# Weight ring below the phase buffers, chained first loads, gate by groups, score matrices inside the mixers, a last tile in halves and a retuned ordering model, on eight Trainium2 cores

## The chip, the cores and the metric

The kernel runs on all 8 cores of one Trainium2 chip (trn2), which lie on two dies (cores 0 to 3 and 4 to 7). Each core computes its own share of the tokens, and no core waits for another. The metric is device microseconds (us) of the slowest core. An execution can fall into a slow state, in which the cores of a die show a lower granted clock (0.83 to 0.98 in the slow runs here, where the others show 0.98 to 0.99). Such runs are named as slow here and are left out of every comparison.

## The reference, cut to what matters

```python
D_MODEL = 1024; SEQ = 8192; BATCH = 2; N_MEM = 256; D_FF = 2816
h = x
for i in range(2):
    n = rms_norm(h, g_mix[i])
    if i == 0:      # A: GLU -> conv over 31 positions -> LayerNorm -> silu; B: gated conv over 3
        h = h + conv_pair_mixer(n, ev_w_in, ..., ev_w_out)
    else:           # u, v = split(gelu(n @ w_in)); y = u * (w_s . layer_norm(v) + b_s); y @ w_out
        h = h + chunked_sgu_mixer(n, od_w_in, ..., od_w_out)
    mem_n = rms_norm(mem, g_mem[i])
    h = h + memory_cross_attention(rms_norm(h, g_xattn[i]), mem_n, w_q, w_k, w_v, w_o)
    h = h + swiglu(rms_norm(h, g_ffn[i]), w_gate, w_up, w_down)
return rms_norm(h, g_final)
```

The attention works on 256 memory tokens, so the kernel folds the query weights into the keys: G = w_q times K, its "score matrix", is built once for each layer, and each token tile multiplies by G.

## The kernel before

Each core holds 2048 tokens in four tiles of 512 (`hT_63` to `hT_66` in the trace; their normalized copies are `nT_67` to `nT_70`). The program is recorded as a list of operations for five engines. A small ordering model then simulates the list and fixes the order on each engine. At run time each engine works strictly in that order.

```python
class Prog:
    AHEAD = {"pe": 6, "act": 32, "dve": 32, "pool": 1, "sp": 1}   # how far an engine may look ahead
    DMA_RATE = 190e3                       # assumed transfer rate, bytes per us
...
            o = min((o for o in go if o.ready <= t + self.SLIP), key=lambda o: (o.due, o.n))
...
            if o.dma is None:
                free[e] = t + o.cost
            else:
                link = max(link, t + 0.8) + o.cost / self.DMA_RATE
                o.done = link + 1.2
```

Weights come as slabs of 512 KB or 1 MB into a ring of memory that lies above the buffers of the running phase. When it is full, it starts again at the phase's border. Slabs are issued from the software queue (POOL), x and small pieces from a hardware queue (SP).

```python
    def ld(self, name, layer, c0):
        ...
        if self.r_ptr + n > SB_LIMIT:
            self.r_ptr = self.r_lo          # border of this phase
...
    def run(...):
        self.load_x(0, "a")                 # all of x at once, halo after tile 0
        for tt in range(1, NT):
            self.load_x(tt, "a")
        self.first_norms()
...
        # conv mixer: LayerNorm and silu write yst; small transfers regroup it as yA
        self.want(("ln", 0))
        self.load_x(1, "b")                 # residual of the later tiles, fetched again
        self.load_x(2, "b")
        self.vproj(0)
...
        # gate of layer 1: tile by tile
        for tt in range(NT):
            for g in range(8):
                ...                         # 4 small matmuls with w_sT, 8 with od_in, gelu, product
        self.kproj(1)
        self.vproj(1)
```

The softmax here doesn't subtract the row's maximum and nothing guards it: scores larger than these inputs give would overflow.

## Time and profile before

| | before |
|---|---|
| time, median of fast runs | 1710.79 us (1709.89 to 1714.03, 4 runs) |
| slowest core of the profiled run | core 4, 1710.6 us |
| TensorE busy | 1592.4 us, 93% |
| table loads on ScalarE | 46, 59.0 us |
| clock granted to the eight cores | 0.981 to 0.985 |

The page's first part gives busy time for each engine. The slices show where TensorE is not full, the windows put numbers on such a stretch, and the list of waits names the tile that TensorE stood still for and what delivered it. In that list, "ACT sqp" and "DVE sqp" are squares from ScalarE and VectorE, which TensorE sums for a norm, and "DMA" is a transfer. The prediction shows these lines.

### The profile page before, as it was taken

The page shows a single profiled execution, that of the slowest core. Times are in us where ns is not written, and L with a number is a line of the kernel's source. Part 1 is how long each engine was busy: PE and PEld are TensorE (multiplying, and loading weights), DVE is VectorE, ACT ScalarE, POOL GpSimd, SP SyncE. Part 2 cuts the span into 40 slices and gives each one's busy share as a digit, 9 for nine tenths or more (in the row PEclk, how much of TensorE's full clock was granted, in tenths as well). Part 3 has the DMA queues.
Part 4 walks back from the last instruction along what each step waited for, and adds up shares of the span by engine and source line. Part 5 has one row for each costly group of instructions (what it writes and reads, how often), then busy time and mean ns, then how long its engine had stood idle before and what let it go on. Part 6 is the DMA issues. An engine that isn't in the chain of part 4 may idle for free.

```text
span 1710.6 us, 23810 instructions; the slowest of 8 cores (1693.8 to 1710.6 us)
## 1 busy us (share of the span) xinstructions
PE 1592.4 (93%) x7799; PEld 752.4 (44%) x7826; DVE 1013.7 (59%) x1636; ACT 708.2 (41%) x1176; POOL 70.1 (4%) x147
## 2 busy tenths in 40 slices
PE   3899895999999999999999897999999999999995
PEld 1444482444444444444444344454444444444442
DVE  1528853665788357673656762474589447683555
ACT  3723364355555043550535422345545134461342
POOL 1000000000000000000000001000000000000000
PEclk9999897999999999999999899999999999999998
DMA  9252248260034355443441208152024436465432
GB/s 202 86 103 38 38 68 192 62 108 4 1 73 82 68 90 96 74 82 66 90 90 25 50 1 133 28 87 50 1 38 80 80 65 121 74 153 118 74 63 99
DMA packets 32376, 130.64 MB, mean 76 GB/s; under 512 B 3584, under 2 KB 10112, under 8 KB 25472
## 3 DMA queue, kind: packets, MB, share of 16 engines
q0 software_dynamic: 18432, 100.03, 33.1%
q1 hardware_dynamic: 13824, 29.08, 5.7%
q8 instruction: 66, 1.08, 0.3%
q14 instruction: 54, 0.44, 0.1%
HBM read 216.51 MB, written 8.39 MB: 131 GB/s over the span
## 4 chain that ended last, share of the span: by engine, by line
PE 84%; DMA 6%; DVE 3%; ACT 3%; issue 2%; SPq 1%; DVEq 0%; ACTq 0%; POOLq 0%
PE ps L595 60%; PE ps L593 21%; DMA hT_65<-x_in 2%; PE ps L107 2%; DMA wbuf_186<-w_od_out 1%; DMA yA_75<-yst 1%; ACT L107 1%; PE ps L1043 1%; DMA wbuf_134<-w_xo 1%; DVE wd L107 1%; DMA wbuf_176<-w_od_in 1%; PE ps L740 1%; DMA wbuf_181<-w_xk 1%; DMA wbuf_175<-w_od_in 1%; SPq L110 0%
## 5 line engine op out<-in xcount | busy, mean ns | idle before, releaser
L107 ACT ACTIVATE ps<-ps 128x512 f32<-128x512 f32 x88 | 50.6, 580 | 216.2 <-PE ps L595 216.1
L595 PE MATMUL ps<-pT,VW 128*128 128x512 f16 x512 | 118.7, 379 | 2.6 <-DVE pT L107 2.6
L107 DVE TENSOR_TENSOR hT_63<-hT_63,ps 128x512 f32<-128x512 f32 x64 | 44.0, 687 | 113.5 <-PE ps L595 111.8
L593 PE MATMUL ps<-tw,sw 128*128 128x512 f16 x352 | 83.5, 379 | 0.8 <-ACT ps L107 0.8
L595 PE MATMUL ps<-tw,sw 128*128 128x512 f16 x352 | 83.5, 379 | 0.6 <-DVE w_0_95 L107 0.6
L107 DVE TENSOR_TENSOR hT_65<-hT_65,ps 128x512 f32<-128x512 f32 x64 | 43.9, 686 | 61.2 <-PE ps L595 61.2
L595 PEld LDWEIGHTS ps<-pT,VW 128*128 128x128 f16 x512 | 50.0, 98 | 63.5 <-issue 3.9
L107 ACT ACT_TABLE_LOAD x46 | 59.0, 1283 | 35.1 <-DVE small L107 10.7
L107 DVE TENSOR_TENSOR hT_64<-hT_64,ps 128x512 f32<-128x512 f32 x64 | 43.9, 685 | 45.9 <-PE ps L595 45.4
L107 DVE TENSOR_TENSOR hT_66<-hT_66,ps 128x512 f32<-128x512 f32 x64 | 43.9, 686 | 45.6 <-PE ps L595 43.5
L107 ACT ACTIVATE pT<-ps,epsc 128x512 f16<-128x512 f32 x64 | 43.7, 683 | 33.1 <-PE ps L595 32.7
L593 PEld LDWEIGHTS ps<-tw,sw 128*128 128x128 f16 x352 | 34.3, 98 | 42.7 <-issue 1.7
L595 PEld LDWEIGHTS ps<-tw,sw 128*128 128x128 f16 x352 | 34.3, 98 | 42.5 <-issue 1.5
L107 ACT ACTIVATE t_2_61<-ps 128x512 f32<-128x512 f32 (+1 forms) x57 | 33.1, 582 | 46.4 <-PE ps L595 41.9
L107 DVE SCALAR_TENSOR_TENSOR nT_67<-hT_63,vec,rs_57 128x512 f16<-128x512 f32 x48 | 34.1, 747 | 28.2 <-ACT sqp_51 L107 26.9
L107 ACT ACTIVATE t_0_59<-ps 128x512 f32<-128x512 f32 (+1 forms) x54 | 31.4, 581 | 40.4 <-PE ps L595 33.2
L595 PE MATMUL ps<-X,wd 128*128 128x256 f16 x288 | 39.3, 285 | 3.6 <-DVE b_ph L107 2.4
L107 DVE TENSOR_TENSOR w_2_97<-ps,w_2_97 128x512 f32<-128x512 f32 x29 | 20.0, 690 | 37.9 <-ACT w_2_97 L107 25.9
L593 PE MATMUL ps<-nT_68,sw 128*128 128x512 f16 x176 | 41.9, 379 | 0.0
L593 PE MATMUL ps<-nT_70,sw 128*128 128x512 f16 x176 | 41.6, 379 | 0.0
L107 DVE TENSOR_TENSOR w_0_95<-ps,w_0_95 128x512 f32<-128x512 f32 x30 | 20.7, 689 | 35.1 <-ACT w_0_95 L107 19.7
L107 DVE TENSOR_TENSOR w_4_99<-ps,w_4_99 128x512 f32<-128x512 f32 x29 | 20.0, 690 | 31.7 <-PE ps L593 16.8
(1249 smaller groups left out, 3371.1 us busy)
## 6 DMA issues: line engine op xcount, KB each, us to landing
hT_64<-x_in SPq DMA_DIRECT2D x8, 512.0 KB, 22.4
hT_65<-x_in SPq DMA_DIRECT2D x8, 512.0 KB, 29.0
hT_66<-x_in SPq DMA_DIRECT2D x8, 512.0 KB, 16.3
X<-a_ph SPq DMA_DIRECT2D x16, 130.0 KB, 6.5
hT_63<-x_in SPq DMA_DIRECT2D x4, 512.0 KB, 10.1
out<-hT_63 SPq DMA_DIRECT2D x4, 512.0 KB, 3.0
out<-hT_64 SPq DMA_DIRECT2D x4, 512.0 KB, 9.9
out<-hT_65 SPq DMA_DIRECT2D x4, 512.0 KB, 3.3
```

Of the source, the lines that this page charges most:

```text
L107: return self.add(eng, lambda e: getattr(e, meth)(**kw), reads, writes, cost=_op_cost(eng, kw))
L593: ins = e.matmul(out, lhsT=l, rhs=r, start=False, stop=(i == np_ - 1), skip_group_check=True)
L595: ins = e.matmul(out, lhsT=l, rhs=r, start=(i == 0), stop=(i == np_ - 1))
L740: ins = e.matmul(self.ps[b][:, i * NMEM:(i + 1) * NMEM], lhsT=ws[i][0](k), rhs=mn[:, k, :], start=(k == 0), stop=(k == KC - 1))
L1043: ins = e.matmul(self.ps[b][:, i * NMEM:(i + 1) * NMEM], lhsT=w(c), rhs=self.kT[:, c, :], start=(hc == 0), stop=(hc == 1))
```

## The change

It is meant to bring data earlier, and to leave TensorE with other work where they are late. It has these parts:

- **Ring:** phase buffers are packed at the top of memory and the ring lies below them from one fixed start. `od_in` is split into `od_v` and `od_u`, and two `od_u` slabs go where K and V of layer 0 were.
- **Start:** the first loads are chained (tile 0, then slabs, then tiles 1, 2, 3). The first four column blocks run chunk by chunk, and VectorE squares every second chunk.
- **yA:** the second fetch of x waits until yA has landed.
- **Gate:** group by group over all tiles, with the K projection in the middle.
- **Scores:** G is built inside the mixers' output projections.
- **Tail:** the last down projection goes tile by tile, the last tile in two halves.
- **Ordering model:** another assumed rate, table loads counted, and table switches put off.

Smaller edits go with these: the norm of the last tile in both mixers is queued after 5 blocks instead of 16, and the attention's products of V and w_o start one step later.

The core of the diff, cut:

```diff
-    DMA_RATE = 190e3
+    TABLES = {AF.Exp: "exp", AF.Ln: "exp", AF.Sigmoid: "sigmoid", AF.Silu: "silu", AF.Gelu_apprx_tanh: "gelu"}
+    TABLE_LOAD = 1.3
+    SWITCH = 4.0
+    DMA_RATE = 320e3
...
-                o = min((o for o in go if o.ready <= t + self.SLIP), key=lambda o: (o.due, o.n))
+                o = min((o for o in go if o.ready <= t + self.SLIP),
+                        key=lambda o: (o.due + (self.SWITCH if o.table not in (None, table) else 0.0), o.n))
...
+                if o.table not in (None, table):
+                    table = o.table
+                    free[e] += self.TABLE_LOAD
...
-        if self.r_ptr + n > SB_LIMIT:
-            self.r_ptr = self.r_lo
+            if self.r_ptr + n > self.r_hi:
+                self.r_ptr = self.r_lo
...
-        for tt in range(1, NT):
-            self.load_x(tt, "a")
+        sl = [self.slab("ev_in", 0, c, None, [self.hT_s[0][2]] if c == 0 else ())[1] for c in (0, 4, 2, 6)]
+        self.load_x(1, "a", [sl[2]])
+        self.load_x(2, "a", [self.hT_s[1][4]])
+        self.load_x(3, "a", [self.hT_s[2][4]])
...
+                if i == 3:
+                    self.load_x(1 + nh, "b", [self.yA_s[nh]])
...
-        self.load_x(1, "b")
-        self.load_x(2, "b")
...
+        for q in range(2):
+            self.slab("od_u", 0, 2 * q, self.kv_lo + q * KC * NMEM * 2)
...
-        for tt in range(NT):
-            for g in range(8):
+        for g in range(4):
+            gate_u(g)
         self.kproj(1)
+        for g in range(4, 8):
+            gate_u(g)
...
+                self.g_step(1, tt, m)      # quarter of G after (1,7), (2,3), (2,7), (3,3)
...
+            if final and h == 1 and part == 1:
+                self.last_down(l, tts, nf) # tile 2 whole, tile 3 in two halves of 256
```

## The prediction

> **What bounds the kernel now.** I read part 1 of the profile page, then the slices, then a table of windows cut at the stage borders, then the list of waits on TensorE and, for the two ends, the timeline.
>
> ```profile
> PE 1592.4 (93%) x7799; PEld 752.4 (44%) x7826; DVE 1013.7 (59%) x1636; ACT 708.2 (41%) x1176; POOL 70.1 (4%) x147
> ...
> PE   3899895999999999999999897999999999999995
> ...
> PEclk9999897999999999999999899999999999999998
> ```
>
> TensorE is busy for 1592.4 of 1710.6 us, so 118 us are idle, and they sit in four places: the first two slices, slices 5 to 7, slices 23 to 25, and the end. The clock digit drops in the same slices. Everywhere else nothing but fewer matmuls could help. The change removes no matmuls, so its worth is the part of those holes that it closes. The windows, whose columns after the length are the busy times of PE, PEld, DVE, ACT and POOL, the granted clock, the DMA share and GB/s:
>
> ```profile
> 10.00:20.00 10.00, 2.28 (x5) 0.42 (x4) 0.00 (x0) 2.30 (x4) 0.00 (x0) 1.00 1.04 199
> 40.00:50.00 10.00, 6.28 (x27) 2.69 (x29) 1.29 (x2) 6.84 (x10) 0.00 (x0) 0.83 0.96 334
> ...
> 160.00:190.00 30.00, 29.68 (x138) 13.34 (x137) 28.51 (x42) 5.78 (x9) 1.05 (x2) 1.00 0.05 6
> ...
> 255.00:273.00 18.00, 4.67 (x43) 3.92 (x41) 6.51 (x7) 7.63 (x12) 1.92 (x4) 0.69 0.91 150
> 273.00:300.00 27.00, 22.08 (x77) 8.84 (x80) 9.05 (x12) 11.37 (x20) 0.00 (x0) 0.82 0.74 206
> ...
> 963.00:997.00 34.00, 25.02 (x134) 11.77 (x133) 20.39 (x34) 9.76 (x16) 1.06 (x2) 0.85 0.35 62
> ...
> 1040.00:1066.00 26.00, 14.76 (x125) 11.41 (x123) 0.69 (x1) 4.97 (x9) 5.28 (x10) 1.00 1.03 159
> ```
>
> In the first 50 us, at 255 and at 1040 the DMA share is near 1 while TensorE waits: these holes are transfers. At 160 DVE is nearly full, so the dip just after it (7 us idle in 190 to 210) is DVE work. The waits name the tiles:
>
> ```profile
> PE ps L595 <- DMA yA_75<-yst: 13.4, 1, 13.4
> ...
> PE ps L595 <- DMA wbuf_176<-w_od_in: 4.1, 1, 4.1
> ...
> PE ps L595 <- DMA wbuf_186<-w_od_out: 2.1, 1, 2.1
> PE ps L740 <- DMA wbuf_183<-w_xv: 1.8, 1, 1.8
> ```
>
> And the end, from the timeline:
>
> ```profile
> 1687.59 2.32 PE L595 MATMUL ps<-hid_93,wbuf_233 128*128 128x512 f16 x10
> ...
> 1699.71 0.58 PE L107 MATMUL ps<-sqp_52,ones 128*128 128x512 bf16 x1 [8.81 <-DVE sqp_52 L107]
> ...
> 1702.18 5.39 DVE L107 SCALAR_TENSOR_TENSOR hT_66<-hT_66,vec,rs_58 128x512 f32<-128x512 f32 x8 [2.62 <-ACT rs_58 L107]
> ```
>
> The last real matmuls end at 1689.9; 20.7 us of final norms and stores follow, and tile 3's statistics wait 8.8 us behind tile 2's scaling on DVE.
>
> **What the Trainium skill says.** "TensorE: Matmul & The Clock Gate", section "Part 1: The HAM clock gate", says that TensorE falls to half clock after an idle window of about 3.4 us and needs about as long busy to recover. The trace agrees: after the wait for yA, four matmuls of 512 columns take 1.71 us (0.43 each), later eight take 1.73 (0.216 each), so each long hole costs about 2 us beyond itself. "DMA: Bandwidth & Descriptors", section "SWDGE vs HWDGE vs iDMA", says that software and hardware queues feed different queues inside each DMA engine, which goes round-robin between them. The trace agrees: tile 0 of x, asked for at 1.5, lands in full only at 21.9 because five weight slabs and the later x tiles share the engines. "ScalarE: Activation LUTs", section "What ACT_TABLE_LOAD costs", gives about 1283 ns for a load; the trace has 46 in 59.0 us (1283 each).
>
> **The change part by part.** One aid first: for each slab I counted in the built order the matmuls from the last reader of the memory it takes to its first use, at the measured 0.216 us per 512 columns. This lead must cover the transfer. A lone slab of 512 KB took 5.0 to 5.2 us from issue (two of the xqT slabs); in a full queue each costs some 3 us more (the three xk slabs issued together took 5.9, 9.0 and 12.1).
>
> *First loads chained.* Before, TensorE does 35.6 us in the first 70; counted up to the second input stage (first matmul at 110.3, 65.7 us of matmul work ahead of it), the start loses 44.6 us, cold clock included. After, x tile 0 (2.1 MB) goes first: at the 334 GB/s of window 40 to 50 that is 6.3 us from about 2.2, so 8.5. Two slabs at 3 us bring the first block to about 15 (the norm, 2 to 3 us after 8.5, lies beside it). Then 2 us for the cold clock. The chunk-wise first block asks 4 x 0.216 = 0.86 us per chunk where DVE scales one in 0.67, so it keeps pace. Tile 0 and the halo last until about 35. Tile 1 needs the two other slabs (6 us) and 2.1 MB more (6.3): landed near 29, normalized by 32. So I expect no second hole: loss 17, of which 2 for table switches on ACT (the order now has 52 of them, all the new ones here or hidden). **Gain 27.**
>
> *Convolution entry.* Same work on DVE (16 builds of 1.3 us amid the gating). Loss 11 to 12 stays. **Gain 0.**
>
> *yA before x.* PE stops at 259.5 and resumes at 273.1, as the last yA pieces queue with 4 MB of x and four slabs; the median piece landed in 2.5 us. After, x waits for yA, so resuming near 262.5: 10.5 us less idle and perhaps 2 of cold clock. The 5 us of waits for squares on ACT right after (1.66 and 2.96 in the timeline) stay. x tile 1 then has 14 us before its add: enough. **Gain 12, up to 17.**
>
> *Ring and gate.* Gate slabs: the lead goes from 3.1 to 56.8 us, because two of the four slabs go into memory of kT and vT and tiles run inside a group. The 9.0 us idle and the clock of 0.85 (5 us) go; v_ln of tile 3 is now wanted only third. I leave 2. **Gain 11.** Then xk and xv: leads of 5 to 8 become 20 to 88, so the 11.2 us idle in 1040 to 1066 go, but the first od_out slab keeps 7.0 us; alone in its queue it needs 5.2. The following 3.4 us in 1066 to 1080 are waits for squares and mostly stay. **Gain 11.** The second v slab keeps its 7.3 us, where it waited 2.3: **gain 0.**
>
> *Score matrices in the mixers.* The 64 matmuls of 256 columns per layer are the same; they move. Gone are the 2.5 and 1.25 us idle at the two attention starts. New: one memory slot for all four slabs, leads 7.1 to 8.0 us against 5.2. **Gain 3.**
>
> *Last tile in halves.* Tile 2's norm and store lie beside tile 3's matmuls. After the last half-group: add 0.5, square 0.5, sum 0.3, Ln and Exp 0.9, eight scalings of 256 columns at 0.41 (as memnT) 3.3, last store 3, hand-overs 1: 9.5 instead of 20.7; the halved groups add 1.5 us of matmul. **Gain 10.**
>
> Sum: 27 + 12 + 11 + 11 + 3 + 10 = 74, so 1710.6 - 74 = 1636.6. The table penalty in the ordering changes little: no loads are saved, and the FFN stages have only some 5 us of idle between them. I say **1636 us**.
>
> **The rivals.** *The start is given back.* Total traffic up to x tile 3 is unchanged and the engines are saturated until 46 us now; if each chained transfer adds an idle 2 us, or slabs come slower than 3 us with x beside them, TensorE starves before tile 1. For it: the DMA share of 1.04. Against it: by count the data are ahead of need. It would cost 8 to 12 us: 1646. *The slot of the score slabs becomes a wait.* For it: the lead is the shortest of all, and the sort of lead (7 us) that waited before. Against it: those waited in a queue five deep, a lone one lands in 5.2. At 2 us each, six times: 12 us, 1648. *DVE takes over.* It now also squares half the first tiles (16 x 0.69 us) while the wd builds fill it at 160 to 190; if the earlier start only makes TensorE wait longer before the convolution, the gain at the start halves: 1650. Against it: that DVE work begins with the second input stage, so it moves along. *It goes better:* yA arrives with the ACT waits gone too and the hole at the gate leaves nothing: 1622.
>
> **Range and chances.** The start (27, give or take 7), yA (12, -4 to +6), the layer 1 stages (22, give or take 5) and the tail (10, give or take 2) are independent, so some 10 us either way with the rivals leaning slow: 1620 to 1654. Slower than 1676 needs three rivals at once. Faster by over 2% 0.96, within 2% 0.035, slower 0.005.
>
> **What would show it.** Right: the first block of matmuls near 15 us and TensorE full from about 20; the wait for yA at 3 us or less; no wait for gate, xk or xv slabs; 9 to 10 us from the last matmul to the end; PE idle near 45 us in all. Wrong: a second hole before 40 us (first rival), waits for xqT slabs in the mixers (second), a longer hole at the convolution (third). If stage lengths match and the time doesn't, my sum has missed a stage.

## The result, and the profile after

The kernel after takes **1647.53 us** (median of 4 fast runs, 1645.15 to 1649.93), against 1710.79 before. The ratio is 0.9627, with a 95% interval of 0.9607 to 0.9647. Ratios here are the mean time of one kernel's fast runs over the mean of the other's fast runs of the same rounds, so they are not quite the ratios of the medians quoted. The profiled run's slowest core is core 5, with 1648.3 us.

The page of the kernel after, parts 1 and 2:

```profile
PE 1587.0 (96%) x7920; PEld 762.0 (46%) x7920; DVE 1025.5 (62%) x1662; ACT 710.9 (43%) x1176; POOL 71.4 (4%) x149
...
PE   5799898999999999999998999999999999999998
...
PEclk9799999999999999999999999999999999999999
```

Idle time of TensorE falls from 118 to 61 us. The dips at yA, at the gate and at the end are nearly gone from the slices, but slices 1 and 2 still have one, with a clock of 7 in the second slice. Four of the waits on TensorE in the kernel after:

```profile
PE ps L813 <- DMA wbuf_109<-w_ev_in: 5.0, 1, 5.0
...
PE ps L619 <- DMA wbuf_175<-w_od_v: 4.2, 1, 4.2
PE ps L619 <- DMA yA_75<-yst: 3.7, 1, 3.7
...
PE ps L1097 <- DMA wbuf_131<-w_xqT: 2.2, 1, 2.2
```

The wait for yA falls from 13.4 to 3.7 us, no xk or xv slab is waited for any more, and the longest wait for a slab is at the start. The windows of the stages that were thin before, now at yA, after it, in the gate and at od_out:

```profile
238.50:256.50 18.00, 14.21 (x128) 12.13 (x127) 11.83 (x22) 11.24 (x21) 2.11 (x4) 1.00 0.62 91
256.50:283.50 27.00, 25.13 (x114) 10.89 (x114) 12.75 (x17) 17.64 (x30) 0.00 (x0) 1.00 0.93 194
942.00:976.00 34.00, 33.15 (x204) 17.05 (x202) 28.14 (x46) 14.10 (x24) 2.11 (x4) 1.00 0.34 63
1000.00:1026.00 26.00, 25.55 (x171) 15.25 (x170) 11.62 (x18) 8.39 (x14) 2.64 (x5) 1.00 0.50 82
```

TensorE is busy 14.2 of 18 us at yA (4.7 before), 25.1 of 27 after it (22.1), 33.2 of 34 in the gate (25.0) and 25.6 of 26 at od_out (14.8). The clock is 1.00 in all four, where before it was 0.69, 0.82, 0.85 and 1.00. The end, from the timeline, with the last real matmuls and the last scalings:

```profile
1637.01 2.35 PE L619 MATMUL ps<-hid_96,wbuf_235 128*128 128x256 f16 x20
...
1642.49 3.26 DVE L110 SCALAR_TENSOR_TENSOR hT_66<-hT_66,vec,rs_57 128x256 f32<-128x256 f32 x8 [0.23 <-ACT rs_57 L110]
```

From the end of those matmuls (1637.01 + 2.35 = 1639.4) to the end of the span are 8.9 us, where it was 20.7.

The start is the surprise. The windows of the first 70 us, first of the kernel before, then of the kernel after:

```profile
0.00:30.00 30.00, 5.57 (x16) 1.67 (x16) 3.07 (x5) 8.32 (x19) 5.71 (x25) 1.00 0.93 176
30.00:70.00 40.00, 30.05 (x166) 12.95 (x169) 13.56 (x31) 28.23 (x45) 0.00 (x0) 0.93 0.51 154
```

```profile
0.00:30.00 30.00, 12.68 (x44) 4.89 (x45) 9.46 (x20) 6.70 (x17) 5.51 (x24) 1.00 0.94 161
30.00:70.00 40.00, 28.91 (x165) 12.89 (x163) 23.33 (x42) 27.04 (x38) 0.53 (x1) 0.79 0.61 164
```

TensorE is busy 12.7 us in the first 30, against 5.6. From 30 to 70 it is busy no longer than before, and at a clock of 0.79 instead of 0.93: what came early is given back. The timeline of the kernel after shows how (lines of TensorE, ScalarE and VectorE):

```profile
22.38 0.58 PE L813 MATMUL ps<-nT_67,wbuf_108 128*128 128x512 f16 x1 [5.02 <-DMA wbuf_109<-w_ev_in]
...
44.21 0.63 ACT L110 ACTIVATE sqp_49<-hT_65 128x512 bf16<-128x512 f32 x1 [5.31 <-DMA hT_65<-x_in]
...
44.99 0.38 PE L110 MATMUL ps<-sqp_49,ones 128*128 128x512 bf16 x1 [2.76 <-ACT sqp_49 L110]
...
47.78 0.62 ACT L110 ACTIVATE rs_57<-t_1_60 128x512 f32<-128x512 f32 x1
...
57.72 0.75 DVE L110 SCALAR_TENSOR_TENSOR nT_68<-hT_64,vec,rs_57 128x512 f16<-128x512 f32 x1
...
58.61 1.86 PE L619 MATMUL ps<-nT_68,wbuf_108 128*128 128x512 f16 x4 [0.37 <-DVE nT_68 L110]
```

Tile 0 starts at 22.4 (34.3 before) because its second slab is late. Tile 1 (`nT_68`) starts at 58.6, not much earlier than before (62.3). From 42 to 58 TensorE has only sums of squares of later tiles and the small matmuls of the halo, and waits for x of the later tiles. But tile 1 itself isn't ready sooner. Its last sum was done at 40.3; then ScalarE stood 5.3 us before a square of tile 2, whose x landed at 44.0, and only after it made tile 1's scale (`rs_57`, done at 48.4). VectorE wrote the eight chunks of `nT_68` between 49.2 and 58.5, with squares of tile 3 between them; before, it wrote them in one go of 5.4 us. On all eight cores TensorE began tile 1 within 0.2 us of the last chunk. So tile 1 waited for its normalization, which the fixed orders of ScalarE and VectorE held behind the squares of tiles whose x came later.

**Where the 63 us come from.** I cut every core's profile at four marks: the first convolution matmul, the first matmul that reads `b_ph` (the output projection after yA), the first that reads `w_sT` (shortly before the gate), and the last that reads `pT` (the end of layer 1's attention). Each mark is the median of the eight cores, and a stage is the difference of two marks, in us. The third column belongs to experiment c1_order_alone below.

| stage | before | after | c1_order_alone | gained by after | gained by c1 |
|---|---|---|---|---|---|
| start to convolution | 194.7 | 185.6 | 186.5 | 9.1 | 8.2 |
| convolution and yA | 78.9 | 67.2 | 66.9 | 11.7 | 12.0 |
| output projection, attention 0, FFN 0, v of layer 1 | 672.9 | 669.6 | 668.4 | 3.3 | 4.5 |
| gate, K, V, od_out, attention 1 | 314.4 | 287.8 | 309.9 | 26.6 | 4.5 |
| FFN 1 and end | 444.2 | 430.8 | 439.8 | 13.4 | 4.4 |
| sum | 1705.1 | 1641.0 | 1671.5 | 64.1 | 33.6 |

Each column is one profiled execution. Taken core by core, the third stage is 673.7, 668.3 and 668.4. Five later kernels that leave the start alone (b1 to b4 and c3) reach the convolution at 183.0 to 185.3. So 2 us in a stage are not to be read.

### The profile page after: what moved, and what is told of

Its sections match the earlier page's. It is cut to its first block, busy times and chain, and to the rows that moved or that the text cites. A ratio compares the mean times of both kernels' runs of the same rounds, so it can differ in the third digit from the quotient of the medians.

```text
span 1648.3 us, 24105 instructions; the slowest of 8 cores (1631.9 to 1648.3 us)
## 1 busy us (share of the span) xinstructions
PE 1587.0 (96%) x7920; PEld 762.0 (46%) x7920; DVE 1025.5 (62%) x1662; ACT 710.9 (43%) x1176; POOL 71.4 (4%) x149
## 4 chain that ended last, share of the span: by engine, by line
PE 88%; DMA 6%; DVE 3%; issue 2%; ACT 1%; SPq 0%; DVEq 0%; POOL 0%; ACTq 0%; POOLq 0%
PE ps L619 62%; PE ps L617 22%; PE ps L110 2%; PE ps L766 1%; PE ps L1097 1%; DMA wbuf_110<-w_ev_in 1%; DMA wbuf_175<-w_od_v 1%; DMA wbuf_149<-w_fgu 1%; DMA hT_64<-x_in 1%; DMA hT_65<-x_in 1%; DMA wbuf_131<-w_xqT 1%; DVE wd L110 1%; DMA yA_75<-yst 1%; DMA wbuf_189<-w_od_out 1%; DMA hT_63<-x_in 0%
## 5 line engine op out<-in xcount | busy, mean ns | idle before, releaser
L110 DVE TENSOR_TENSOR hT_63<-hT_63,ps 128x512 f32<-128x512 f32 x64 | 44.0, 687 | 73.8 <-PE ps L619 73.6
L110 ACT ACT_TABLE_LOAD x52 | 66.7, 1283 | 32.5 <-DVE small L110 10.5
L110 DVE TENSOR_TENSOR hT_65<-hT_65,ps 128x512 f32<-128x512 f32 x64 | 43.9, 686 | 53.9 <-PE ps L619 53.7
L110 DVE TENSOR_TENSOR hT_64<-hT_64,ps 128x512 f32<-128x512 f32 x64 | 43.9, 685 | 47.7 <-PE ps L619 47.3
L110 DVE TENSOR_TENSOR hT_66<-hT_66,ps 128x512 f32<-128x512 f32 (+1 forms) x72 | 45.1, 626 | 44.5 <-PE ps L619 41.6
L110 ACT ACTIVATE pT<-ps,epsc 128x512 f16<-128x512 f32 x64 | 43.7, 683 | 28.9 <-PE ps L619 27.8
L110 ACT ACTIVATE t_2_61<-ps 128x512 f32<-128x512 f32 (+1 forms) x56 | 32.6, 582 | 43.5 <-PE ps L619 26.0
L110 ACT ACTIVATE t_0_59<-ps 128x512 f32<-128x512 f32 (+1 forms) x54 | 31.4, 581 | 40.2 <-PE ps L619 24.6
L110 DVE TENSOR_TENSOR w_2_99<-ps,w_2_99 128x512 f32<-128x512 f32 x29 | 20.0, 690 | 25.7 <-ACT w_2_99 L110 13.2
L110 DVE SCALAR_TENSOR_TENSOR nT_67<-hT_63,vec,rs_57 128x512 f16<-128x512 f32 x48 | 34.2, 746 | 2.9 <-ACT sqp_49 L110 2.9
L110 ACT ACTIVATE t_1_60<-ps 128x512 f32<-128x512 f32 (+1 forms) x42 | 24.6, 585 | 26.5 <-PE ps L619 20.6
L110 DVE SCALAR_TENSOR_TENSOR nT_69<-hT_65,vec,rs_57 128x512 f16<-128x512 f32 x40 | 28.7, 745 | 9.6 <-ACT rs_57 L110 9.6
```

Of the source, the lines that this page charges most:

```text
L110: o = self.add(eng, lambda e: getattr(e, meth)(**kw), reads, writes, cost=_op_cost(eng, kw))
```

## The experiments

All outputs are right. All runs were timed beside the kernel before on the same chip. Before's fast runs had means of 1708.8 to 1709.0 us there and 1711.4 beside the kernel after, so kernels of different batches are best compared by their ratios. "Against after" below is the ratio less 0.9627, times 1710.8. The intervals are some 0.002 either way (more for a1, a3, c1 and c2), or 3 to 4 us, and a difference of two such ratios is known to some 5. So a4, b2 and b3 are not told from zero by their ratios.

| run | median of fast runs, us | ratio (95%) | against after, us |
|---|---|---|---|
| a1_order | 1658.51 | 0.9723 (0.9682 to 0.9765) | +16 |
| a2_rate | 1655.62 | 0.9686 (0.9667 to 0.9705) | +10 |
| a3_no_chain | 1652.37 (1649.47 to 1661.98) | 0.9682 (0.9634 to 0.9729) | +9 |
| a4_old_start | 1648.29 | 0.9646 (0.9627 to 0.9665) | +3 |
| b1_no_halves | 1653.82 | 0.9679 (0.9660 to 0.9698) | +9 |
| b2_x_before_yA | 1647.26 | 0.9640 (0.9616 to 0.9663) | +2 |
| b3_gate_by_tile | 1650.18 | 0.9657 (0.9638 to 0.9676) | +5 |
| b4_scores_back | 1656.74 | 0.9693 (0.9676 to 0.9709) | +11 |
| c1_order_alone | 1679.79 | 0.9851 (0.9807 to 0.9894) | |
| c2_rate_alone | 1698.68 | 0.9963 (0.9914 to 1.0011) | |
| c3_od_v_first | 1642.64 and 1643.82, two fast runs | none given | |
| c4_od_v_rate420 | 1650.13 | 0.9660 (0.9645 to 0.9675) | +6 |

**My theory after the result** was that the start failed because TensorE and ScalarE stand in a fixed order behind squares and sums of later tiles, and that the rest went as predicted. The rivals were that the chain itself is what costs, that DVE has become the limit, and that part of the gain does not come from the moved loads at all but from the ordering model, which I had written off.

### a1_order: the later tiles' squares moved back in the order

```diff
-    DMA_RATE = 320e3
+    DMA_RATE = 190e3
...
+            lag = 20 if j is js[2] else 29 if j is js[3] else 0
-                    self.push(j.key, lambda k=k, j=j: j.sq(k), 0)
+                    self.push(j.key, lambda k=k, j=j: j.sq(k), lag)
```

> The changed kernel with its transfers untouched; only the order moves: the sums of squares of x tiles 2 and 3 are put into the program after the first blocks of tile 1, and the ordering model's transfer rate goes back to 190 GB/s. Theory 1 (the start gains only 5 of the expected 27 us because TensorE and ScalarE, which work strictly in order, stand behind sums of squares of x tiles that land later): tile 1 starts near 44 instead of 58.6 us, and the time falls by 10 to 14 us against the changed kernel, to about 1635. Theory 2 (the chained transfers bring the data too late, whatever the order): tile 1 still starts after 55 and the time stays at 1647.

Its fast runs took 1658.30, 1658.51 and 1668.24 us, slower than after. Tile 1 began at 51.6, not at 44 (again within 0.2 us of its normalized copy on all cores), and the convolution at 196.5 (median of the cores) instead of 185.6. Two of the waits on TensorE in this run:

```profile
PE ps L619 <- DVE nT L110: 7.2, 2, 5.2
PE ps L619 <- DVE a_ph L110: 6.1, 2, 5.9
```

The waits moved to DVE, and the late sums came late. All the engines work in a fixed order, so putting one kind of work back holds others up. My theory as stated, with its gain of 10 to 14 us, falls. As the edit changed two things at once, the next run has one of them; the later squares with the new rate were not run.

### a2_rate: only the assumed transfer rate

```diff
-    DMA_RATE = 320e3
+    DMA_RATE = 190e3
```

> The changed kernel with only the ordering model's transfer rate back at 190 GB/s. It moves tile 1's statistics ahead of the squares of tile 2 on ScalarE but leaves the sums of tiles 2 and 3 ahead of tile 1 on TensorE. Theory 1 expects a part of the gain only, 2 to 6 us, with the remaining wait on the sums of tile 2 and 3; theory 2 expects nothing.

With one constant of the ordering model put back, the time rises by 8 us by the medians (10 by the ratios) and the convolution begins at 194.4, as before (194.7), although the chained loads are all still there. The chain is worth nothing without the order that the new rate gives. In this run it is TensorE's own order that holds tile 1: by the medians of the cores its normalized copy was done at 54.2, and its matmuls began at 64.5. In a1, at the same rate with the squares moved back, the copy was done at 51.3 and the matmuls began at 51.4, 5 us before after's 56.4, and yet the convolution began later (196.5). So an early tile 1 alone does not bring the convolution forward.

### a3_no_chain and a4_old_start: the loads of the start

```diff
-        self.load_x(1, "a", [sl[2]])
-        self.load_x(2, "a", [self.hT_s[1][4]])
-        self.load_x(3, "a", [self.hT_s[2][4]])
+        self.load_x(1, "a")
+        self.load_x(2, "a")
+        self.load_x(3, "a")
```

a4_old_start also takes out the chunk-wise first block and the squares on DVE, so the whole start is written as before, with the new ordering model.

> The changed kernel with every first load issued at once, as the kernel before does; chunk-wise first block and split squares stay. Theory 2 (chained transfers arrive late) expects it to be faster by 5 to 10 us, with x tile 3 landed at 46 rather than 58 us. Theory 1 expects a later first block (26 instead of 22.4 us), but tiles 2 and 3 of x earlier, so their sums hold TensorE less: within 5 us of the changed kernel either way.

> The changed kernel with the whole start of the kernel before: nothing chained, squares on ScalarE alone, no chunk-wise first block. It measures what the start part is worth in the time: the stage borders of the two profiles say 5 to 7 us (1653 to 1655); my prediction had said 27 (1674).

a3 had three slow runs of six, and its profiled run had a lower clock on two cores, so its time says little. Its cores reached the convolution at 188.4, not earlier than after's 185.6, so the chain is not what costs. a4 is clean: its fast runs were 1647.82, 1648.29 and 1649.57 us, and the convolution began at 187.1. The hand-made part of the start, to which I had given 27 us, is worth 1 us by the medians of the fast runs (3 by the ratios, with intervals that overlap). VectorE as the limit, the other rival, was not run alone.

### b1_no_halves: the last down projection as before

```diff
-            if final and h == 1 and part == 1:
+            if False:
```

> The changed kernel with the last down projection as in the kernel before (both tiles under each weight slab, whole tiles). If the tail is worth what the two profiles show from the last matmul to the end (20.7 against 9.1 us, less 1.5 us of added matmul), it is slower by 10 us: 1657. If the tail's gain were lost elsewhere, it would stay at 1647.

1653.82 us: 6 us by the medians and 9 by the ratios. The last stage took 439.6 instead of 430.8 us, which is 8.8. The part does what it is meant to do.

### b2_x_before_yA: the second fetch of x at its old place

```diff
-                if i == 3:
-                    self.load_x(1 + nh, "b", [self.yA_s[nh]])
...
+        self.load_x(1, "b")
+        self.load_x(2, "b")
```

> The changed kernel with the second load of x tiles 1 and 2 issued where the kernel before does it, with no wait for the yA pieces. If the wait for yA shrank from 13.4 to 3.7 us because x goes behind it, the wait comes back at 11 to 14 us and the time rises by 10 us: 1657. Rival: the wait shrank because the weight slabs beside it go earlier or ScalarE orders its work otherwise; then the time stays within 3 us.

1647.26 us in the fast runs, the same as after, and the wait for yA was 3.2 us. So x was not what yA waited for, although the stage did gain what I had predicted. The trace of the kernel before could have told: SP issues x only after the last yA piece (259.82 against 259.02). In b2 too it comes some 0.8 us behind that piece, which lands in 5.5 to 8.0 us over the eight cores, no later than in after (5.8 to 8.5), where x waits. Something else in the change had moved yA.

### b3_gate_by_tile: the gate in the old order, with the new memory

```diff
-        for g in range(4):
-            gate_u(g)
+        for tt in range(NT):
+            for g in range(8):
+                gate_u(g, tt)
         self.kproj(1)
-        for g in range(4, 8):
-            gate_u(g)
```

> The changed kernel with the gate tile by tile, as before, and the key projection after it, with memory as changed (two gate slabs in the memory of kT and vT). If the order by groups is what pays, by freeing ring memory early for the xk and xv slabs, their waits come back: slower by 8 to 12 us, 1656 to 1660. If it is only the memory (early gate slabs), the gate starts without a wait and the time rises by 3 us at most.

1650.18 us in the fast runs, so 3 by the medians (5 by the ratios). Two of its waits on TensorE, which the kernel after does not have at this size:

```profile
PE ps L766 <- DMA wbuf<-w_xv: 5.8, 4, 1.9
...
PE ps L619 <- DMA wbuf<-w_od_out: 2.2, 1, 2.2
```

The stage took 293.5 us, against 287.8 in after (287.9 to 289.4 in b1, b2, b4 and c3) and 309.9 where only the order is new. So some 6 of the 22 us between those two go when the gate's order is undone, the K projection in its middle with it. The other 16 stay, and they belong to the new memory and what else moved in that stage.

### b4_scores_back: G built in the attention, as before

```diff
-        if q is not None:
-            self.g_part(l, q)
+        return
...
+        for q in range(4):
+            self.g_part(l, q)
```

> The changed kernel with the score matrices built at the start of the attention, their slabs in the ring, as before. I expected 3 us for this part; the two profiles show a wait of 2.2 us for one xqT slab that the part itself has brought. If the part is worth 3 us or more: 1650 or more. If the slot's wait eats it: 1646 to 1648.

1656.74 us: 9 by the medians, 11 by the ratios, where I had said 3. Two of its waits on TensorE:

```profile
PE ps L619 <- DMA wbuf<-w_fgu: 11.0, 1, 11.0
...
PE ps L619 <- DVE G L110: 2.7, 2, 1.4
```

The wait for G is what the part was to remove, and it has the size of before (2.5). The 11.0 us are something else: with G's slabs in the ring, the slabs of the FFN take other places in it, and one of them is then late. That wait is neither in before nor in after. It belongs to the undoing, not to what the part is worth. Against c1_order_alone, the third stage of after has gained nothing (669.6 and 668.4). So the 9 are more than the part brought, and its own worth is probably nearer to the 3; no run here has it alone.

### c1_order_alone and c2_rate_alone: the ordering model in the kernel before

By the medians, undoing the parts one at a time had explained some 27 of the 63 us, and nothing moved by hand explained yA. So the last question was turned round: what does the ordering model alone do to the kernel before?

```diff
 # c2: only this line;  c1: this, and the table lines of the change
-    DMA_RATE = 190e3
+    DMA_RATE = 320e3
 # c1 only
+    TABLE_LOAD = 1.3
+    SWITCH = 4.0
```

> The kernel before with nothing of the change but its ordering model (the assumed transfer rate of 320 instead of 190, the table load of 1.3 us counted, a table switch delayed by 4 us): no load, tile or memory is moved by hand. Theory: the gains at the convolution entry (7 to 9 us) and at yA (about 10 us) come from the ordering and not from the chained loads or from x behind yA. Then 1690 to 1698 us, the convolution begins at 186 to 188 instead of 194.7, and the wait for yA falls from 13.4 to 5 or less. Rival: the order helps only together with the moved loads and memory of the change; then 1707 to 1712 and the wait for yA stays above 10.

> The kernel before with one constant changed, the assumed transfer rate. If the rate is what moves the start (tile 0's blocks come ahead of the later tiles' sums of squares) and the table accounting is what moves yA: convolution entry 186 to 188, wait for yA still above 9, 1700 to 1704 us. If the rate does both: as c1, 1690 to 1698. If it does nothing without the rest: 1708 to 1712.

c1 took **1679.79 us against 1708.93**: 29 us, almost half of the whole gain, with no load, tile or buffer moved by hand, and more than the theory asked for. (One of its four runs, 1695.21, had a clock of 0.972 on two cores. It is in the ratio, so the ratio understates the gain.) c2 took 1698.68 us, 10 less than before. (One of its runs, 1715.71, had a clock of 0.968 on two cores, and with it the interval of the ratio reaches 1. The profiled spans, 1692.2 against 1705.0 by the medians of the cores, speak for a gain.) In the stage table, c1 has the whole gain of the kernel after up to the end of yA.

For yA the issue times tell why. The transfers of yA and one line of POOL's slab issues, first in the kernel before, then in c1 (L114 and L119: ns min/median/max that an issue takes, first and last issue in us; below each, the time from issue to landing; the POOL line: start in us, duration, what is loaded):

```profile
L114 SPq DMA_DIRECT2D yA_75<-yst x16: 585/602/2034, 242.9 to 259.0; - x16
...
DMA to landing us min/median/max: 2.1/2.5/14.0
...
258.52 0.53 POOL L110 DMA_DIRECT2D wbuf_129<-w_ev_out  x1 [1.22 <-PE ps L740]
```

```profile
L119 SPq DMA_DIRECT2D yA<-yst x16: 585/602/877, 232.9 to 246.8; - x16
...
DMA to landing us min/median/max: 2.1/2.3/7.3
...
246.66 0.53 POOL L115 DMA_DIRECT2D wbuf<-w_ev_out  x1 [21.64 <-PE ps L110]
...
PE ps L604 <- DMA yA<-yst: 2.7, 1, 2.7
```

Before, the last pieces of yA are issued up to 259.0, after three weight slabs (254.81, 256.77 and 258.52), and the slowest takes 14.0 us. In c1 the last piece is issued at 246.8, with the first slab (246.66), and the slowest takes 7.3. Counted from the first convolution matmul, the first slab is issued at 59 us in both (and in after), while the last piece moves from 63 to 59. By these times, 4 us of order decide whether small transfers go ahead of the slabs or behind them. All eight cores agree: in before and in c2, four of the sixteen pieces are issued after the first slab, and in c1 and in after, one. In the kernel after they are issued the same way (last piece 247.8, first slab 247.83, slowest 8.5). In c2, with the rate alone, yA still waits:

```profile
PE ps L595 <- DMA yA<-yst: 13.6, 1, 13.6
```

So it is the table lines of the ordering model that move yA, not the rate. Which of them, the counted load or the delayed switch, was not run. The start needs both: the convolution begins at 191.6 in c2 and at 186.5 in c1. The windows of c1's first 70 us:

```profile
0.00:30.00 30.00, 5.53 (x16) 1.66 (x16) 3.23 (x5) 8.21 (x19) 5.71 (x25) 1.00 0.93 185
30.00:70.00 40.00, 35.22 (x198) 15.58 (x199) 15.77 (x37) 30.42 (x49) 0.00 (x0) 1.00 0.49 147
```

c1 begins no earlier than before (5.5 us busy up to 30). Then it is busy 35.2 of 40 us at full clock, where after is busy 28.9 at 0.79. Two different starts reach the convolution within 1 us of each other.

### c3_od_v_first and c4_od_v_rate420: trying for more

```diff
 # both
-            self.slab("od_u", 0, 2 * q, self.kv_lo + q * KC * NMEM * 2)
+            self.slab("od_u", 0, 2 * q, self.kv_lo + q * KC * NMEM * 2, [self.slab("od_v", 0, 4)[1]])
 # c4 only
-    DMA_RATE = 320e3
+    DMA_RATE = 420e3
```

> The kernel after, but the gate's slabs wait in their queue until the second v slab has landed, so that this one is alone. It waited 4.2 us with four slabs behind it. If those four share its rate, its landing falls from 10.9 to about 6 us, the wait goes, and the time is 2 to 4 us less than after's 1647.5: 1643.5 to 1646. Rival: it is late because it is asked for late, whatever stands behind it: 1647 to 1648.5, wait above 3 us.

> c3 with the assumed transfer rate of the ordering at 420 instead of 320, which puts still more of tile 0's blocks ahead of tile 1's sums of squares. If 190 to 320 won 8 us because TensorE's fixed order stood behind late sums, 420 wins some 1 to 4 us more at the start: 1640 to 1644, convolution entry at 182 to 184. Rival: the real rate at the start is below 420, the order now puts sums before work whose data come later, and it is a matter of chance: 1646 to 1655.

c3's two fast runs, 1642.64 and 1643.82 us, are the shortest times of any kernel here. The other two were slow (one die at 0.88 to 0.92), so no interval was given. The time is at the lower edge of what was expected, but the mechanism was met only in part. The transfers issued around that moment:

```profile
wbuf<-w_od_v POOLq DMA_DIRECT2D x1, 1024.0 KB, 8.7
wbuf<-w_od_u POOLq DMA_DIRECT2D x2, 512.0 KB, 7.2
```

The slab still takes 8.7 us with no other slab behind it (10.8 in after; over the eight cores 8.5 to 9.6 against 8.6 to 10.8). My 6 us were read from slabs of 512 KB, and this one is 1 MB. The wait was 1.9 to 3.1 us over the eight cores, against 2.1 to 4.2, and the third stage was 3.0 us shorter by the medians. The first two stages were 2.9 us shorter as well, where nothing was moved by hand. c3 is probably the better kernel, by 2 to 5 us, but with two runs that is not settled.

c4 took 1649.6 to 1653.6 us in its fast runs, and its convolution began at 189.6, later than in after. The rival's time holds: a higher assumed rate is not better. From 190 to 320 the start gains; from 320 to 420 it loses 5.6 us (189.6 against c3's 184.0), and the whole some 7. The rival's reason was not traced.

## Why the prediction was right or wrong

The total held: 1636 was predicted, with a range of 1620 to 1654, and 1647.5 came. The sum was 74, the stages gave 64. By its steps:

- **"First loads chained", gain 27: this step failed.** The stage gained 9.1 us. The failing sentences are "Two slabs at 3 us bring the first block to about 15" and "landed near 29, normalized by 32. So I expect no second hole". Tile 0 of x landed at 12.9, not at 8.5: the sum took the 334 GB/s of window 40 to 50, although the same table has 199 at a DMA share of 1.04 in 10 to 20. The two slabs, issued at 10.4 and 11.0, landed at 18.8 and 22.1. Tile 1 of x was issued at 25.5, after the third slab, and landed at 33 to 38, and tile 3 landed at 58, where before it had landed by 53. The first block began at 22.4. Tile 1 was normalized at 58.5, not by 32, and the second hole came, from 42 to 58. It took the clock with it: 0.50 from 46.2 until 63.3. I had counted only whether the data would be there, and that too early, and not which squares stood ahead of tile 1's normalization in the orders of ScalarE and VectorE. My first rival, "The start is given back" (1646), is what happened, for this further reason. With the old rate in the ordering the chained start gains nothing (a2_rate); without the chain the new order gains nearly all of it (a4, c1).
- **"Convolution entry", gain 0: right.** In the 50.7 us around the entry TensorE idled 7.4 us before and 7.5 after.
- **"yA before x", gain 12: the size was right (11.7), the cause wrong.** Putting x back costs nothing measurable (b2), and the ordering alone removes the wait (c1). "The last yA pieces queue with 4 MB of x and four slabs" named both suspects, and I picked x. By the issue times, the slabs issued ahead of the pieces were the ones; x stood behind them.
- **"Ring and gate", 11 and 11: right within the margin.** (The gate's own terms, 9 + 5 - 2, make 12.) Together with 1.25 for G in attention 1 these were 23, and the stage gained 26.6. Of these, 4.5 come with the order alone, and the other 22 do not: in c1 TensorE still waits 6.0 us for a gate slab of od_in and 8.3 for xk and xv. The second v slab kept its wait, and a little more than I said (2.3 before, 4.2 after, on the slowest cores).
- **"Score matrices in the mixers", gain 3: not refuted.** The 9 to 11 of b4 contain a new 11.0 us wait that undoing brings in. The second rival showed itself only once, as 2.2 us at the second xqT slab.
- **"Last tile in halves", gain 10: right, with a shift.** Halves are worth 8.8 us of the last stage, and the ordering gives 4.4 more. In part of that last, c1 squares tile 3 before the table switch instead of after it, so its sum no longer waits 8.8 us behind tile 2's scalings.
- **"The table penalty in the ordering changes little": this step failed too.** I looked only for table loads saved. There are indeed none (52 loads now, 66.7 us), but the counting reorders ScalarE everywhere. The ordering model as a whole is worth 29 us, of which the rate alone is perhaps 10.

So the largest term was 18 us too high, and the range held because the other stages came 8 us above their terms, with help from an ordering that I had left out. That the total came so near is in part luck: two errors offset each other. The signs agree: no gate, xk or xv wait and 8.9 us at the end, as said, but 61 us of idle TensorE instead of 45.

What stays open: the 4.5 us that the order gains in each of the third and fourth stages were not traced to single waits. The 16 us of the fourth stage that are neither the order nor the gate's sequence were not split between the memory of the early slabs, the ring, G inside od_out and the smaller edits. And the parts undone one by one sum to some 40 us by the ratios, with overlaps both ways, so no list of single worths adds up to 63.

## What to carry to other kernels

Where a model fixes each engine's order, run its constants alone on the old kernel before crediting any hand-made move: here they carried almost half of the whole gain, and nearly all of what the first two stages gained. When a load is brought forward, check what stands ahead of its consumers in the order of every engine on the way, and what the transfers that it pushed back will hold up. Undoing a part of a finished change measures the new waits of the undoing as well, so do the part alone too.

## What the Trainium skill lacked or had wrong

- **"TensorE: Matmul & The Clock Gate", "Part 1: The HAM clock gate":** the page says that about 3.4 us of sustained work bring the full clock back. It doesn't say how busy a window must be. In the kernel after the clock fell to 0.50 at 46.2 us, inside the second of two waits of 2.76 and 1.73 us, each shorter than its idle window. It stayed at 0.50 until 63.3, although TensorE was busy 9.7 of the 14.5 us from 47.5 to 62.
- **"ScalarE: Activation LUTs", "What ACT_TABLE_LOAD costs":** its 1283 ns for a load agree with the trace (52 loads in 66.7 us). Its further 1380 ns of drain don't show here: one ACTIVATE ends at 225.54, the load starts at 225.55, and the next ACTIVATE starts at 226.85, so this switch takes 1.31 us and not 2.66. After each of the 52 loads the next ACTIVATE starts within 0.02 us.
- **"DMA: Bandwidth & Descriptors", "Bandwidth":** the page gives 6.15 us for 1 MB, without the time to emit descriptors and with the pair's other core idle. It has no figure from issue to landing with all cores at work: here 1 MB with no other slab behind it took 8.7 us (8.5 to 9.6 over the eight cores), and a lone 512 KB took 5.0 to 5.2.
- **No page that I used** has a figure for a small transfer behind large ones from the other queue. A 64 KB piece landed in 2.1 to 2.5 us as a rule, and in up to 14.0 when it was issued after three 512 KB slabs (259.02 to 272.97 in the kernel before).
